# Scores of a neighbourhood attention as three split-format matmuls instead of one in full precision

## The chip, the cores and the metric

The kernel runs on one core of a Trainium2 chip. The metric is the device time of one execution in microseconds (us), as the median of several runs. The engines are named as in the profile: PE (TensorE matmuls), PEld (its weight loads), DVE (VectorE), ACT (ScalarE), POOL (GpSimd), SP (SyncE, which issues most DMAs).

## What is computed

One layer of an encoder on 512 tokens (a grid of 8 rows by 64 columns) with 2048 channels, in float32. The normalised input is projected to five parts: value and gate of a convolution group (group a, 1024 channels), and queries, keys and values of a 2-D neighbourhood attention (16 heads of 64 channels). The outputs of both groups are normalised, projected together and added to the input; a gated FFN of width 5632 follows. The part that the change concerns is

```python
scores = jnp.einsum("bchd,bicjhd->bchij", q_row, k_win).astype(jnp.float32)
scores = scores + jnp.transpose(bias, (2, 0, 1, 3))[None]
p = jax.nn.softmax(scores.reshape(b, GRID_W, h, kh * kw), axis=-1)
return jnp.einsum("bchij,bicjhd->bchd", p, v_win)
```

where a token sees all 8 rows and a window of 16 columns, and q is scaled by 1/8.

## The kernel before

**Layout and products.** Channels lie on the 128 partitions, tokens on the free axis (512). A large product is made in the split format: each factor is the sum of a high part, rounded to the format fp32r, and a low part, and three matmuls hi\*hi, hi\*lo, lo\*hi are added in PSUM (`mm3`, lines 126 to 128, one weight block of 128x128 against 512 tokens). Weights come by DMA in units of 8 blocks (`raw`, 128x1024, seven buffers, issued by SP three units ahead); `parts` makes the high part with ACT (`whi`, line 115) and the low part with DVE (`wlo`, line 116), with four buffers each. So a whi or wlo waits until PE is done with the unit four before, and PE waits for it if it is late.

**Stages.** `ORDER` (line 51, `"aavaav" + "aq" * 4 + "qqqq"`) says what is projected in turn: a pair of value and gate tiles of the convolution ("a"), half of the attention's values ("v"), or queries and keys of one pair of heads ("q", eight pairs). Then `out_half` projects the outputs of group a (products `po2`, shown as po), later those of the attention, and the FFN follows (from about 690 us on). A projected tile takes two weight units of 24 matmuls. After each unit, `tick` (line 133) moves two hand-written generators on by one step: `attention` (line 525) and, from pair 4 on, `group_a` (line 390). The instructions of a step may not be issued before that unit's last matmul. Beyond that and the pinned sequences, the scheduler of the language sets each engine's order when the kernel is built, by priorities and by when it reckons that inputs are ready; each engine then works through its list in that fixed order.

**Attention of a pair** (two heads of 64 channels, on partitions 0 to 63 and 64 to 127). `project_qk` (line 427) projects q and k; DVE empties the PSUM banks, times the token's norm (lines 433 and 437, the latter with the keys in another order of tokens). `scores` (line 465): eight matmuls, four column blocks b by two heads, each contracting 64 rows, with 128 queries against 256 keys, in full precision, pinned one behind the other (line 472; the trace shows each as two instructions). `softmax` (line 479) adds the bias table that a DMA has brought (DVE, line 482), and takes maximum, exponential (ACT, line 487) and quotient (DVE, line 489, `tab`). `turn` transposes the result on PE (line 499, `trp`), ACT empties it (line 504, `pt`). `values` (line 507) multiplies by the values into the PSUM bank with the tag "po"; ACT copies it out as `ao` (line 520) and squares it (`sq`, line 168) for the attention's norm.

**Group a.** `group_a` sums the eight convolved tiles y on DVE (`acc`, line 396), gets the mean by a matmul with ones (`st`, line 399), subtracts it (line 404), normalises twice, and makes the split operands `ma`. `rsqrt_steps` (line 171) makes a token's norm and spreads it over the partitions by two matmuls on diagonal matrices (`st<-dg,ones`, line 218), which ACT copies out (line 220, named after the norm: `ra` for group a's second one). These `st` use the bank "po" too, of which there is one. `read_a` (line 593) empties the first products of `out_half` once `ra` is there: DVE multiplies by it (`oa`, line 598) and adds to the residual (line 599). There are three banks for such products (`psm`, "mm"), so the fourth product waits for the first to be emptied.

Of the kernel before, what the change touches and what calls it, by code (L numbers as in the profile page):

```python
# [10 lines left out]
F32 = mybir.dt.float32  # L11
F32R = mybir.dt.float32r
AF = mybir.ActivationFunctionType
# [3 lines left out]
P = 128  # L17
# [49 lines left out]
def layer(ctx: ExitStack, tc: tile.TileContext, xT, xG, w_in, w_v, w_out, w_up, w_down, par, tab, out):  # L67
    nc = tc.nc
# [16 lines left out]
    def t2(name, dt=F32):  # L85
        return tp.tile([P, S], dt, tag="t2k", name=name)
# [5 lines left out]
    pin = tc.keep_in_program_order  # L92
# [170 lines left out]
    for k in range(KD):  # L263
        x1.append(t2("x"))
        last = pin(nc.sync.dma_start(x1[k], xG[k]))
        h, l = t2("xh", F32R), t2("xl", F32R)
# [35 lines left out]
    def project(n):  # L302
        ps = psm.tile([P, S], F32, tag="mm", name="pj")
        for u in range(KD // U):
            w = weights()
            for k in range(U):
                kk = u * U + k
                m = mm3(ps, w, k, xs[kk][0], xs[kk][1], kk == 0, kk == KD - 1)
            tick(m)
            while late and rstd:  # L310
                late.pop(0)()
        return ps
# [114 lines left out]
    def project_qk(p):  # L427
        got = []
        for j, nm in enumerate("qk"):
            ps = project(2 * NC_ + j * NP_ + p)  # L430
            t = t2(nm)
            if nm == "q":
                nc.vector.tensor_mul(t, ps, rstd[0])
            else:

                by = "p (i j c) -> p j i c"
                nc.vector.tensor_mul(t.rearrange("p (j i c) -> p j i c", i=NB, j=2), ps.rearrange(by, i=NB, j=2),
                                     rstd[0].rearrange(by, i=NB, j=2))
            got.append(t)
        qk.append(got)  # L440

    def keys(k, b):

        if b in (0, NB - 1):
            w = k.rearrange("p (j c) -> p j c", j=2)[:, :, b and P:(b and P) + P]
        else:
            w = k[:, b * 64:b * 64 + 384].rearrange("p (j c) -> p j c", j=2)[:, :, :P]
        return w.rearrange("p j (i c) -> p i j c", i=2)
# [5 lines left out]
    hps = [slice(j * DH, (j + 1) * DH) for j in range(2)]  # L454
# [10 lines left out]
    def scores(p, first):  # L465
        q, k = qk[p]
        wide = psa.tile([P, 2, 2, 2 * P], F32, tag="sc", name="sc")
        banks = [wide[:, j] for j in range(2)]
        banks += [psa.tile([P, 2, 2 * P], F32, tag="tr", name="sc", bufs=2) for _ in range(2)]
        for b in range(NB):  # L470
            for j, hp in enumerate(hps):
                m = nc.tensor.matmul(banks[b // 2 * 2 + j][:, b % 2, :], q[hp, b * P:(b + 1) * P],
                                     keys(k, b)[hp], start=True, stop=True)
                if not first:
                    pin(m)
                first = False
        return banks

    def softmax(banks, ts):
# [45 lines left out]
    def attention():  # L525

        before = None
        for p in range(NP_):
            while len(qk) <= p:
                yield  # L530
            ts = tables(p)
            yield
            if before:
                values(*before)
            banks = scores(p, not before)
            softmax(banks, ts)
            yield
            yield
            yield
            pts = turn(ts)  # L540
            yield
            before = p, pts
        yield
        values(*before)
        yield

    p, n = -1, 0
    for step in ORDER:
        if step == "a":
            if n < 2:  # L550
                with tc.issue_after(last.ins):
                    glu(n)
            else:
                glu(n)
            n += 1
            continue
        if step == "v":
            project_v(len(vg))
            continue
        p += 1  # L560
        project_qk(p)
        if p == 0:
            steps.append(attention())
        if p == NORM_AT:
            asteps.append(group_a())
# [439 lines left out]
```

## Time and profile before

| what | us |
|---|---|
| median of 3 runs | 2044.64 (2043.89 to 2045.69) |
| profiled execution | 2047.1 |
| its span (first to last instruction) | 2045.3 |
| PE busy in it | 2025.5 |
| DVE busy | 1672.8 |
| ACT busy | 1035.4 |
| scores of pair 0 start | 237.7 |
| scores of pair 7 end | about 527 |
| granted clock of TensorE, mean | 0.996 |

The page and its views come from one profiled execution, which is a little longer than the median. A line of a timeline reads: start, duration (both us), engine, line of the kernel, operation, output<-inputs, shape and type, number of instructions; then, in brackets, how long the engine sat idle before it and what it waited for. Of matmuls, which are pipelined, the time from start to start is what one costs; the duration also holds the pipeline's depth. A group line ends with the busy time of the group, the mean duration in ns, and the idle time before its members. A line of windows reads: stretch, its length, busy us and number of instructions for each engine, granted clock (1.00 is full), busy share of the DMA engines, GB/s.

### The profile page before, as it was taken

What the parts mean: (1) busy time and instruction counts of PE and PEld (TensorE: products, weight loads), DVE (VectorE), ACT (ScalarE), POOL (GpSimd) and SP (SyncE); (2) the same over time, 40 slices, a digit from 0 to 9 for tenths busy, and PEclk for the clock granted to TensorE, in tenths of its full rate; (3) what the DMA queues carried; (4) which work ended last, traced back from release to release, by engine and by line L of the source; (5) the groups of instructions that cost most, each with busy time, mean ns of one, the idle gap of its engine ahead of it and who ended that gap; (6) DMA issues with size and microseconds to landing.
All of it is one profiled execution on the core that took longest, in us unless ns stands there. A gap on an engine that the chain in (4) does not pass through costs nothing.

```text
span 2045.3 us, 28399 instructions
## 1 busy us (share of the span) xinstructions
PE 2025.5 (99%) x10752; PEld 1731.9 (85%) x10752; DVE 1672.8 (82%) x2319; ACT 1035.4 (51%) x1662; POOL 156.2 (8%) x186
## 2 busy tenths in 40 slices
PE   9999999999999999999999999999999999999997
PEld 7888888878888898888888888888888888888887
DVE  7986888878577898888888788788888888889876
ACT  6323234347346555555555555555554555555552
POOL 0000000000001001111111111111111111110110
PEclk9999999999999999999999999999999999999998
DMA  7232333336347435566566565665555566555682
GB/s 254 82 104 91 114 95 103 108 119 216 104 121 178 113 114 144 118 151 145 124 144 144 135 133 145 138 134 142 131 146 143 124 146 146 130 134 127 149 212 83
DMA packets 97209, 275.38 MB, mean 135 GB/s; under 512 B 10928, under 2 KB 11696, under 8 KB 97072
## 3 DMA queue, kind: packets, MB, share of 16 engines
q1 hardware_dynamic: 71712, 227.40, 36.6%
q0 software_dynamic: 25216, 46.15, 15.6%
q8 instruction: 85, 1.39, 0.3%
q14 instruction: 52, 0.43, 0.1%
q10 hardware_dynamic: 144, 0.01, 0.0%
HBM read 218.99 MB, written 54.53 MB: 134 GB/s over the span
## 4 chain that ended last, share of the span: by engine, by line
PE 95%; DVE 2%; ACT 1%; DMA 1%; issue 1%; SPq 0%; DVEq 0%; ACTq 0%
PE pu L723 25%; PE pu L728 13%; PE pd L128 8%; PE pd L126 8%; PE pd L127 8%; PE pj L128 5%; PE pj L127 5%; PE pj L126 5%; PE po L126 3%; PE po L127 3%; PE po L128 3%; PE pv L330 1%; PE pv L332 1%; PE pv L331 1%; PE pu L126 1%; PE pu L128 1%
## 5 line engine op out<-in xcount | busy, mean ns | idle before, releaser
L115 ACT ACTIVATE whi<-raw 128x1024 fp32r<-128x1024 f32 x364 | 384.9, 1059 | 506.2 <-PE pj L127 148.0
L116 DVE TENSOR_TENSOR wlo<-raw,whi 128x1024 fp32r<-128x1024 f32 x364 | 443.9, 1221 | 215.6 <-ACT whi L115 205.9
L723 PE MATMUL pu<-xc,whi 128*128 128x512 f32 x2240 | 574.9, 392 | 0.2 <-ACT pl L735 0.2
L723 PEld LDWEIGHTS pu<-xc,whi 128*128 128x128 f32 x2240 | 409.2, 189 | 74.3 <-ACT pl L735 0.5
L728 PEld LDWEIGHTS pu<-xc,wlo 128*128 128x128 f32 x2240 | 305.6, 190 | 21.9
L728 PE MATMUL pu<-xc,wlo 128*128 128x256 f32 x2240 | 312.3, 282 | 0.0
L128 PE MATMUL pd<-hh,wlo 128*128 128x512 f32 x640 | 249.2, 391 | 0.0
L127 PE MATMUL pd<-hl,whi 128*128 128x512 f32 x640 | 249.2, 389 | 0.0
L126 PE MATMUL pd<-hh,whi 128*128 128x512 f32 x640 | 248.9, 391 | 0.0
L842 POOL DMA_DIRECT2D x2d<-pdc x160 | 139.2, 872 | 1169.6 <-ACT pdc L841 1051.5
L127 PE MATMUL pj<-xl,whi 128*128 128x512 f32 x512 | 200.4, 391 | 0.1
L128 PE MATMUL pj<-xh,wlo 128*128 128x512 f32 x512 | 200.0, 391 | 0.0
L126 PE MATMUL pj<-xh,whi 128*128 128x512 f32 x512 | 198.6, 392 | 0.4 <-ACT xh L267 0.4
L735 ACT ACTIVATE pl<-pu 128x256 f32<-128x256 f32 x280 | 104.4, 382 | 168.6 <-PE pu L723 168.5
L115 ACT ACTIVATE whi<-ws 128x1024 fp32r<-128x1024 f32 x132 | 139.6, 1058 | 76.9 <-PE pu L723 55.3
L384 DVE SCALAR_TENSOR_TENSOR y<-ch,prm,y 128x500 f32<-128x500 f32 (+14 forms) x240 | 173.4, 741 | 4.5
L116 DVE TENSOR_TENSOR wlo<-ws,whi 128x1024 fp32r<-128x1024 f32 x132 | 160.8, 1218 | 19.7 <-ACT whi L115 19.6
L128 PEld LDWEIGHTS pd<-hh,wlo 128*128 128x128 f32 x640 | 120.1, 188 | 28.8 <-DVE wlo L116 3.0
L127 PEld LDWEIGHTS pd<-hl,whi 128*128 128x128 f32 x640 | 120.3, 188 | 25.0
L126 PEld LDWEIGHTS pd<-hh,whi 128*128 128x128 f32 x640 | 120.5, 188 | 21.9
L841 ACT ACTIVATE pdc<-pd 128x512 f32<-128x512 f32 x160 | 93.8, 588 | 84.1 <-PE pd L128 84.1
L126 PEld LDWEIGHTS pj<-xh,whi 128*128 128x128 f32 x512 | 96.0, 188 | 22.3 <-issue 1.7
(188 smaller groups left out, 2911.3 us busy)
## 6 DMA issues: line engine op xcount, KB each, us to landing
raw<-in_w_up SPq DMA_DIRECT2D x176, 512.0 KB, 3.7
raw<-in_w_down SPq DMA_DIRECT2D x88, 512.0 KB, 4.0
x2d<-pdc POOLq DMA_DIRECT2D x160, 256.0 KB, 4.8
raw<-in_w_in SPq DMA_DIRECT2D x60, 512.0 KB, 3.7
raw<-in_w_out SPq DMA_DIRECT2D x32, 512.0 KB, 3.7
raw<-in_w_v SPq DMA_DIRECT2D x16, 512.0 KB, 4.0
tab<-in_tab SPq DMA_DIRECT2D x32, 256.0 KB, 5.1
x<-in_xG SPq DMA_DIRECT2D x16, 256.0 KB, 5.3
```

The costliest lines, as they stand in the source:

```text
L115: i = nc.scalar.activation(hi[:, :n], raw[:, :n], AF.Copy)
L116: j = nc.vector.tensor_sub(lo[:, :n], raw[:, :n], hi[:, :n].bitcast(F32))
L126: nc.tensor.matmul(ps, hi[:, a], mh, start=start, stop=False)
L127: nc.tensor.matmul(ps, hi[:, a], ml, start=False, stop=False)
L128: return nc.tensor.matmul(ps, lo[:, a], mh, start=False, stop=stop)
L330: nc.tensor.matmul(ps, xh, wh[:, f], start=kk == 0, stop=False)
L384: nc.vector.scalar_tensor_tensor(y[:, a:b], h[:, a + j - PAD:b + j - PAD], prm[:, o + j:o + j + 1], y[:, a:b], op0=ALU.mult, op1=ALU.add)
L723: return nc.tensor.matmul(ps, w[0][:, k * P:(k + 1) * P], comb[c][k], start=k == 0, stop=k == U - 1)
L728: nc.tensor.matmul(ps[:, H:], w[1][:, k * P:(k + 1) * P], comb[c][k][:, :H], start=False, stop=False)
L735: nc.scalar.activation(to, ps, AF.Copy)
L841: nc.scalar.activation(t, ps, AF.Copy)
L842: nc.gpsimd.dma_start(xd[d], t, accum_op=ALU.add)
```

## The change

After the eviction of q and of k, ACT copies the tile to a high part in fp32r and DVE subtracts it from the tile for a low part (16 copies and 16 subtractions of 128x512 in all). Each score matmul becomes three: high keys by high queries, low keys by high queries, high keys by low queries, added in PSUM. The part is the outer loop, the head the inner, so a pair has 24 matmuls of 64 rows instead of 8 in full precision. Softmax and all else stay as they are. Lines behind the first edit have numbers higher by 3, lines behind the second by 5.

```diff
@@ project_qk
-            got.append(t)
+            h, l = t2(nm + "h", F32R), t2(nm + "l", F32R)
+            nc.scalar.activation(h, t, AF.Copy)
+            nc.vector.tensor_sub(l, t, h.bitcast(F32))
+            got.append((h, l))
         qk.append(got)
@@ scores
         for b in range(NB):
-            for j, hp in enumerate(hps):
-                m = nc.tensor.matmul(banks[b // 2 * 2 + j][:, b % 2, :], q[hp, b * P:(b + 1) * P],
-                                     keys(k, b)[hp], start=True, stop=True)
-                if not first:
-                    pin(m)
-                first = False
+            at = slice(b * P, (b + 1) * P)
+            for part, (x, y) in enumerate(((0, 0), (0, 1), (1, 0))):
+                for j, hp in enumerate(hps):
+                    m = nc.tensor.matmul(banks[b // 2 * 2 + j][:, b % 2, :], q[x][hp, at], keys(k[y], b)[hp],
+                                         start=part == 0, stop=part == 2)
+                    if not first:
+                        pin(m)
+                    first = False
         return banks
```

## The prediction

> **What bounds the kernel now.** I read the page first: how busy each engine is, then the chain that ended last.
>
> ```profile
> span 2045.3 us, 28399 instructions
> ...
> PE 2025.5 (99%) x10752; PEld 1731.9 (85%) x10752; DVE 1672.8 (82%) x2319; ACT 1035.4 (51%) x1662; POOL 156.2 (8%) x186
> ...
> PE 95%; DVE 2%; ACT 1%; DMA 1%; issue 1%; SPq 0%; DVEq 0%; ACTq 0%
> ```
>
> PE is busy for 99% of the span and carries 95% of the chain. So time saved on PE is saved in the end, unless PE then waits for something that was just in time before. DVE at 82% is the likely source of such waits. ACT at 51% is the second, since it runs in a fixed order. The sum is made against the profiled execution (2047.1 us, of which 2045.3 are the span and 1.8 lie around it); it is 2.5 us (0.12%) above the median of 2044.64, so I take the differences from it and put them on the median. About 0.2% (4.1 us) can be told from no change here: faster is under 2040.5, slower over 2048.7.
>
> **1. The scores themselves.** The first fence has PE's timeline around the scores of pair 0, then the view of line 472 by itself. Then come two slices of PE's warm-up (line 258: split-format matmuls of 64 rows, 256 and 512 columns, two halves of the array in turn) and a group row.
>
> ```profile
> 237.35 0.39 PE L128 MATMUL pj<-xh,wlo 128*128 128x512 f32 x1
> 237.67 2.00 PE L472 MATMUL sc<-k,q 64*128 64x256 f32 x16
> 239.60 0.50 PE L126 MATMUL pj<-xh,whi 128*128 128x512 f32 x1
> ```
>
> ```profile
> L472 PE MATMUL sc<-k,q x128: 376/376/480, 237.7 to 526.8; 64*128 64x256 f32 x128
> ```
>
> ```profile
> 5.20:5.32 0.12, 0.12 (x6) 0.12 (x4) 1.00 0.87 341
> 5.32:5.44 0.12, 0.12 (x6) 0.12 (x4) 1.00 1.02 393
> ```
>
> ```profile
> L728 PE MATMUL pu<-xc,wlo 128*128 128x256 f32 x2240 | 312.3, 282 | 0.0
> ```
>
> A pair has 8 matmuls in the program, and the trace shows 16: one in full precision is two instructions. They run as eight groups of two, one for each head, which lie beside each other: (2.00 - 0.48) / 7 = 0.217 us from group to group. The block holds PE for 239.60 - 237.67 = 1.93 us, of which 8 x 0.217 = 1.73 is this cadence and 0.2 is entering and leaving. After the change there are 24 instructions in twelve groups of two. No row shows such a group, so its price is bounded. Split-format 64-row matmuls moved on by one group per 0.12 us in the warm-up; I take 0.119. The line of 128x256 gives 312.3 / 2240 = 0.139 at worst, and half of the old cadence, 0.108, is the other end. So a block takes 12 x 0.119 + 0.2 = 1.63 us: 0.30 less per pair, and 2.4 us over eight pairs (ends: 0.06 less, 0.43 less). I take the warm-up, as it has the same 64 rows and both halves of the array.
>
> The Trainium skill ("FP8 and Floating Point Precision", TensorE Precision Notes) counts four passes for full precision; three instead of four would save a quarter of the 1.73, or 3.5 us in all, by my estimate from that page. The trace gives 0.217 for four passes, 0.054 each, while the warm-up pays 0.119 for one group, so it is against the whole quarter.
>
> **2. The copies and subtractions.** The groups below are the nearest to them; then come a stretch of projections (busy time of PE, PEld, DVE, ACT, POOL) and DVE's timeline.
>
> ```profile
> L267 ACT ACTIVATE xh<-x,g 128x512 fp32r<-128x512 f32 x16 | 11.0, 725 | 3.3 <-DMA x<-in_xG 2.2 <-DMA g<-in_par 1.1
> L268 DVE SCALAR_TENSOR_TENSOR xl<-x,g,xh 128x512 fp32r<-128x512 f32 x16 | 11.2, 749 | 5.5 <-ACT xh L267 5.4
> ```
>
> ```profile
> 200.00:250.00 50.00, 50.00 (x229) 40.98 (x228) 42.24 (x59) 14.41 (x26) 0.00 (x0) 1.00 0.37 111
> ```
>
> ```profile
> 227.37 0.68 DVE L437 TENSOR_TENSOR k<-pj,rstd 128x512 f32<-128x512 f32 x1
> ...
> 418.44 1.22 DVE L116 TENSOR_TENSOR wlo<-raw,whi 128x1024 fp32r<-128x1024 f32 x1 [4.21 <-ACT whi L115]
> ```
>
> Sixteen copies at about 0.7 us on ACT and sixteen subtractions at 0.7 on DVE make 11 us on each, 1.4 per pair. In a 50-us stretch, about a pair, DVE has 7.8 us free and ACT over 30. The scores need the low part of k, but the eviction of k in pair 0 ends at 228.05 and its scores start at 237.67: 9.6 us of cover for a copy and a subtraction. I cost this at nothing. Without the cover, a wait on it would be 1.4 us per pair.
>
> **3. What moves.** In the built program the score blocks and what follows them stand at other places among the weight matmuls. Counting those from the scores of pair 4: the mean of group a (line 399) stands behind 52 of them instead of 49, the scores of pair 5 at 142 instead of 127, the first transposes at 194 instead of 192, the norm of group a (line 218, its second use) behind 288 instead of 280. Up to pair 4, PE has no wait in this stage. Then there were two:
>
> ```profile
> 432.31 0.39 PE L126 MATMUL pj<-xh,whi 128*128 128x512 f32 x1
> 434.02 1.10 PE L399 MATMUL st<-acc,ones 128*128 128x512 f32 x2 [1.32 <-DVE acc L396]
> ...
> 478.87 0.39 PE L127 MATMUL pj<-xl,whi 128*128 128x512 f32 x1
> 480.17 0.63 PE L499 MATMUL trp<-ident,tab 128*128 128x128 f32 x4 [0.91 <-DVE tab L489]
> ...
> 481.77 0.40 PE L128 MATMUL pj<-xh,wlo 128*128 128x512 f32 x1
> ```
>
> ```profile
> 432.46 1.41 DVE L396 TENSOR_TENSOR acc<-acc,y 128x512 f32<-128x512 f32 x2
> ...
> 480.54 1.22 DVE L116 TENSOR_TENSOR wlo<-raw,whi 128x1024 fp32r<-128x1024 f32 x1
> ```
>
> Wait A costs 434.02 - 432.31 - 0.23 = 1.48 us. It ends when DVE has its sum, whatever PE does. Three weight matmuls more ahead of it (3 x 0.227, the time between neighbours) give PE 0.68 us of work that was waiting; pair 4's 0.30 goes into that wait. Wait B costs 480.17 - 478.87 - 0.23 = 1.07; with the scores of pair 5 further back, the transposes have their input in time, and it goes. But at 481.77 a matmul starts just as the wlo of 480.54 ends (481.76): with B gone this weight part is late next, and I put 0.33 on it (bounds 0 and 1.07). The gain ahead of the norm is then 6 x 0.30 + 0.68 + 1.07 - 0.33 = 3.2 us (six pairs, without the fourth). Loads on SP's queue move too: bias tables of pair 6 by two weight loads, x by two; in my walk each still lands before its reader, the tables of pair 6 with the least to spare. I cost that at nothing; if they come late, the transposes of pair 6 are late by as much.
>
> **4. The new wait, C.** Here the norm of group a moves, on PE and against ACT's queue. PE, then ACT, then DVE, in before:
>
> ```profile
> 502.62 0.64 PE L218 MATMUL st<-dg,ones 128*128 128x512 f32 x2
> 503.10 0.40 PE L127 MATMUL po<-mal,whi 128*128 128x512 f32 x1
> ...
> 504.49 0.40 PE L127 MATMUL po<-mal,whi 128*128 128x512 f32 x1
> ...
> 504.95 0.39 PE L126 MATMUL po<-mah,whi 128*128 128x512 f32 x1
> ```
>
> ```profile
> 498.96 1.06 ACT L115 ACTIVATE whi<-raw 128x1024 fp32r<-128x1024 f32 x1 [1.10 <-PE po L127]
> 499.93 0.49 ACT L487 ACTIVATE tab<-tab,nm 128x256 f32<-128x256 f32 x1
> ...
> 501.90 0.58 ACT L520 ACTIVATE ao<-po 128x512 f32<-128x512 f32 x1
> ...
> 503.30 0.60 ACT L220 ACTIVATE ra<-st 128x512 f32<-128x512 f32 x1 [0.15 <-PE st L218]
> 504.92 1.06 ACT L115 ACTIVATE whi<-raw 128x1024 fp32r<-128x1024 f32 x1 [1.03 <-PE po L127]
> ```
>
> ```profile
> 503.93 1.29 DVE L598 TENSOR_TENSOR oa<-po,ra 128x512 f32<-128x512 f32 x2
> ```
>
> The norm's matmuls (st) write the one bank that ACT's ao (line 520) empties, and in before that was done 0.14 us ahead (502.48 against 502.62). ACT then made ra, DVE used it to empty a product bank (503.93 and half of 1.29: 504.6), and the matmul at 504.95 that needed the bank came 0.35 later. All margins just held. In the built after, ACT's order is turned: the whi of 504.92, which waits for the matmul of 504.49, stands ahead of ao, sq and ra, not behind them. And st stands one matmul behind the one that this whi waits for; directly behind st comes the matmul that needs the emptied bank. Let T be the time at which st would start (504.95 by before's clock). whi starts at T - 0.03; the next on ACT 0.97 later (498.96 to 499.93), so ao ends at T + 0.94 + 0.58 = T + 1.52. st starts 0.14 later at T + 1.66, ra 0.68 behind it (502.62 to 503.30) and ends at T + 2.94, oa needs 0.03 + 0.69, and PE goes on at about T + 3.8. Undisturbed it would be T + 0.48 (502.62 to 503.10). The wait costs 3.3 us: the lead of 3.2 is gone, and pair 7's 0.30 is left.
>
> **5. The clock.** PE's work is thin for these 3.8 us: two idle stretches of 1.7 with two matmuls between them. Something like it is in before, at the start of the FFN:
>
> ```profile
> 691.06 0.28 PE L128 MATMUL pu<-xc,wlo 128*128 128x256 f32 x1
> 692.47 1.01 PE L218 MATMUL st<-dg,ones 128*128 128x512 f32 x2 [1.14 <-DVE dg L213]
> 694.17 0.39 PE L126 MATMUL pu<-xc,whi 128*128 128x256 f32 x1 [0.69 <-ACT rstd L220]
> ```
>
> ```profile
> 692.00:696.00 4.00, 2.79 (x12) 0.82 0.21 80
> 696.00:700.00 4.00, 4.00 (x28) 0.75 0.00 0
> ```
>
> (The last rows: busy PE, granted clock, DMA.) Behind it the granted clock was 0.5 for (0.18 + 0.25) x 4 / 0.5 = 3.4 us, worth at most half of that, 1.7 us. At waits A and B, shorter, the clock stayed at 1.00. C is the longer kind, so I expect such a stretch and take 1.5 us (ends: 0 and 1.7).
>
> The Trainium skill ("TensorE: Matmul & The Clock Gate", Part 1) has the clock drop after one idle window of about 3.4 us. The trace shows a drop with gaps of 1.14 and 0.69 around two matmuls; a wholly idle window isn't needed.
>
> **The sum:** -3.2 - 0.3 + 3.3 + 1.5 = +1.3: 2044.64 + 1.3 = **2046.0 us** (span 2046.6, profiled 2048.4).
>
> **Rivals.**
> - *C without a drop of the clock*: 2044.64 - 0.2 = 2044.5. For it: the two gaps of C are split by two matmuls, as idle stretches A and B were short. Against it: the drop at 694. By the skill's rule on a wholly idle window it would be this one.
> - *C doesn't bite*: ACT runs early enough, or the chip's margins at the norm differ from my walk. Then the lead stays: 2044.64 - 3.5 = 2041.1, and with the low cadence (12 x 0.011 x 8 = 1.1 more) 2040.0, which is faster. Against it: whi waits for PE's own progress, so no lead of PE's changes the order.
> - *The heads do not lie side by side* in the new groups, which is the slower side: 24 instructions one after the other at 0.119 are 2.86 instead of 1.43 us per pair, 11.4 us in all: 2057. It is slower than before from 0.149 us per group on (2.9 us over 96 groups beyond 0.119); at 0.139 the time is 2047.9. Speaking for it: each group has its own weights to load, 24 per pair instead of 16. Against it: the warm-up's slices.
>
> **How the numbers follow.** C with the clock: 0.40, 2046.0. C without: 0.25, 2044.5. C not biting: 0.17, about half of it under 2040.5. Slower groups, or a wait that I have not found, over 2048.7: 0.18. So faster 0.09, same 0.40 + 0.25 + 0.08 = 0.73, slower 0.18. The range reaches from C not biting with the low cadence (2040.0) to the forecast with 0.139 (+1.9), the dearest clock (+0.2) and the weight part's bound (+0.7): 2040.0 to 2048.8; it leaves out some 0.18.
>
> **What would show it.** In after: a score block of 24 instructions that lasts 1.6 us; no waits of scores on the low parts; wait A shorter by 0.7, B gone; at the second st (line 218 there too) an idle time of about 1.7 us that ao ends, then one of 1.6 that oa ends; and a slice with a granted clock under 1 behind it. The prediction is wrong if the block takes 2 us or more, if st doesn't wait for ao, or if PE waits at places that have none now.

## The result, and the profile after

On one chip the kernel before took 2045.68 us (median of 12 runs, 2043.89 to 2046.76) and the changed kernel 2049.78 (12 runs, 2045.52 to 2052.68). The ratio is 1.0018, with an interval of 1.001 to 1.0026. The change makes the kernel slower, by some 4 us. As a ratio that is a little under the 0.2% below which the prediction spoke of no change, but the interval excludes 1, and the time lies over the 2048.7 from which it spoke of slower, and 1.0 us above the upper end of the range. Of the 3.8 us between the forecast of 2046.0 and this time, 1.0 lies in the base: the three runs that the prediction started from have a median of 2044.64, the twelve here one of 2045.68. The runs of the changed kernel spread over 7 us, those of the kernel before over 3: that is a finding too, and it comes back below.

The profiled execution took 2052.57 us; so it is one of the longer ones. Two lines of its page, the span and the chain by engine:

```profile
span 2050.8 us, 28563 instructions
...
PE 93%; DVE 3%; DMA 2%; issue 1%; ACT 1%; DVEq 0%; ACTq 0%
```

PE still carries nearly all of the chain, but the DMAs' share went from 1% to 2%. The span is 2050.8 - 2045.3 = 5.5 us longer than before. To see where this arises, I followed the same matmuls through both traces. PE's timeline at the scores of pair 0:

```profile
237.37 0.39 PE L477 MATMUL sc<-kh,qh 64*128 64x256 f32 x2
237.59 0.28 PE L477 MATMUL sc<-kl,qh 64*128 64x256 f32 x2
237.71 0.28 PE L477 MATMUL sc<-kh,ql 64*128 64x256 f32 x2
...
238.78 0.28 PE L477 MATMUL sc<-kh,ql 64*128 64x256 f32 x2
238.99 0.50 PE L126 MATMUL pj<-xh,whi 128*128 128x512 f32 x1
```

Each score row is a group of two, one matmul for each head. There are twelve, and from the second to the last it is (238.78 - 237.59) / 10 = 0.119 us from group to group. The block holds PE for 238.99 - 237.37 = 1.62 us, against 1.93 before. (This execution is 0.30 us ahead here already; that is its start, not the change.) The waits of PE between 400 and 540 us, all of them (in total, times, longest):

```profile
PE po L126 <- DVE oa L603: 1.4, 1, 1.4
PE st L218 <- ACT ao L525: 1.4, 1, 1.4
PE st L399 <- DVE acc L396: 0.9, 1, 0.9
```

Wait A is 0.9 us instead of 1.3, wait B is gone, and two new ones stand at the place called C. PE's timeline there, then ACT's, one row of DVE's and two windows (PE, PEld, DVE, ACT, POOL, clock, DMA):

```profile
500.30 0.39 PE L127 MATMUL po<-mal,whi 128*128 128x512 f32 x1
...
502.32 0.73 PE L218 MATMUL st<-dg,ones 128*128 128x512 f32 x2 [1.41 <-ACT ao L525]
504.47 0.50 PE L126 MATMUL po<-mah,whi 128*128 128x512 f32 x1 [1.41 <-DVE oa L603]
...
505.53 0.63 PE L126 MATMUL po<-mah,whi 128*128 128x512 f32 x1
505.95 0.63 PE L127 MATMUL po<-mal,whi 128*128 128x512 f32 x1
```

```profile
500.73 1.06 ACT L115 ACTIVATE whi<-raw 128x1024 fp32r<-128x1024 f32 x1 [0.20 <-PE po L127]
501.69 0.58 ACT L525 ACTIVATE ao<-po 128x512 f32<-128x512 f32 x1
...
503.09 0.60 ACT L220 ACTIVATE ra<-st 128x512 f32<-128x512 f32 x1 [0.16 <-PE st L218]
```

```profile
503.72 1.28 DVE L603 TENSOR_TENSOR oa<-po,ra 128x512 f32<-128x512 f32 x2
```

```profile
502.00:506.00 4.00, 2.27 (x7) 1.49 (x8) 4.00 (x7) 1.50 (x3) 0.00 (x0) 0.87 1.06 396
506.00:508.00 2.00, 2.00 (x6) 1.60 (x5) 1.50 (x3) 0.00 (x0) 0.00 (x0) 0.50 0.78 303
```

The matmul of 500.30 ran at 504.49 before: 4.19 us ahead, of which 0.48 is the norm that before had already done and 0.30 the earlier start, so the lead is 3.4. Then whi, ao, st, ra, oa follow one another as the prediction walked them. The matmul of 504.47 ran at 504.95 before: 0.2 us of the lead is left. Behind it neighbours are 0.42 apart instead of 0.23, at half the clock, and behind pair 7's scores the lead has turned into a lag:

```profile
528.07 0.50 PE L126 MATMUL po<-mah,whi 128*128 128x512 f32 x1
```

That matmul started at 527.12 before, so the lag is 0.95 us, or 1.25 without the earlier start; the prediction's sum has 1.3. From here to 633 us every engine runs 0.95 behind. The rest, 5.5 - 0.95 = 4.5 us, arises at the start of the FFN, for which the prediction's sum has no term. DVE's timeline there, before and then after:

```profile
633.34 1.23 DVE L673 TENSOR_TENSOR ws<-raw 128x1024 f32<-128x1024 f32 x1
```

```profile
636.32 1.23 DVE L678 TENSOR_TENSOR ws<-raw 128x1024 f32<-128x1024 f32 x1 [2.06 <-DMA raw<-in_w_up]
```

`ws` is the first sum of two weight blocks of the FFN. It reads a load that SP issues. SP's timeline and the DMA view (KB, us from issue to landing) of this one load, before and then after:

```profile
628.39 0.33 SPq L110 DMA_DIRECT2D raw<-in_w_up  x1
```

```profile
raw<-in_w_up SPq DMA_DIRECT2D x1, 512.0 KB, 4.9
```

```profile
629.34 0.33 SPq L110 DMA_DIRECT2D raw<-in_w_up  x1
```

```profile
raw<-in_w_up SPq DMA_DIRECT2D x1, 512.0 KB, 6.9
```

Before, the load landed at 633.3, just as DVE came to it at 633.34: a margin of less than 0.1 us, which no row of waits shows, as the row has no idle time. After, it took 2 us more. Behind `ws` on DVE stand the low parts `xc` of the FFN's input and a low weight part. DVE itself has slack here: before, it waited 7.8 us for PE between 628 and 690 us, after only 2.5. But SP issues a next load only when DVE has made the weight part that frees the buffer. The next load of these weights left at 643.23 instead of 640.25, and DVE's waits for such loads grew (in total, times, longest; before and then after):

```profile
DVE raw L675 <- DMA raw<-in_w_up: 1.2, 2, 0.6
```

```profile
DVE raw L680 <- DMA raw<-in_w_up: 5.5, 2, 2.8
```

So DVE's lag of 3.0 us lasts up to the last `xc`, for which PE waited 0.77 us in before already. The matmul that waits is the 44th of the FFN; the first starts at 674.20 before (so the FFN begins there, and not at about 690) and at 675.14 after. PE, before and after, and the windows of after:

```profile
680.28 0.39 PE L126 MATMUL pu<-xc,whi 128*128 128x256 f32 x1 [0.77 <-ACT xc L612]
```

```profile
683.32 0.58 PE L126 MATMUL pu<-xc,whi 128*128 128x256 f32 x1 [2.86 <-ACT xc L617]
```

```profile
682.00:686.00 4.00, 2.68 (x12) 2.68 (x13) 3.22 (x10) 3.15 (x9) 0.00 (x0) 0.55 0.84 212
686.00:690.00 4.00, 4.00 (x24) 4.00 (x23) 3.88 (x4) 1.95 (x5) 0.00 (x0) 0.59 0.17 58
```

The lag is 683.32 - 680.28 = 3.04 us. Behind this wait the clock was halved for (0.45 + 0.41) x 4 / 0.5 = 6.9 us, which is worth at most 3.4; matched matmuls lag by 5.6 behind it, and what follows gives back 0.7 and takes again 0.5. Up to the last 20 us this execution ran at half clock for 13.7 us in all (3.4 behind C, 6.8 here, 3.4 behind 699), that of the kernel before for 3.4.

### The profile page after: what moved, and what is told of

It is laid out like the page before. It is cut to its first block, busy times and chain, and to the rows that moved or that the text cites. A ratio compares the mean times of both kernels' runs of the same rounds, so it can differ in the third digit from the quotient of the medians.

```text
span 2050.8 us, 28563 instructions
## 1 busy us (share of the span) xinstructions
PE 2027.6 (99%) x10816; PEld 1735.9 (85%) x10816; DVE 1681.5 (82%) x2335; ACT 1046.1 (51%) x1678; POOL 156.6 (8%) x186
## 4 chain that ended last, share of the span: by engine, by line
PE 93%; DVE 3%; DMA 2%; issue 1%; ACT 1%; DVEq 0%; ACTq 0%
PE pu L728 25%; PE pu L733 13%; PE pd L128 8%; PE pd L126 8%; PE pd L127 8%; PE pj L126 6%; PE pj L128 6%; PE pj L127 6%; PE po L126 2%; PE po L128 2%; PE po L127 2%; DMA raw<-in_w_up 2%; PE pv L332 1%; PE pv L331 1%; PE pv L330 1%; PE pu L126 1%
```

## The experiments

Two theories stood at first. **M**: the prediction's mechanism (C and the clock behind it) takes the lead, and this is the whole of what is regular. **L**: the load at the FFN's start is late because of the change, and its wait is the larger part. Each batch ran on one chip beside runs of the kernel before. Diffs are against the changed kernel unless said otherwise.

### e1: the changed kernel again

> The changed kernel once more, not altered, to see how its time spreads and what its profile shows when it is short. Theory M (the moved order makes the wait C and a stretch of half clock behind it; what comes on top is a load of FFN weights that lands late in some executions): runs fall in two groups, about 2045 to 2047 and 2048 to 2053. If this profile is of the short group, C is there all the same (two gaps of 1.4 us at the second st), but the first pu matmul of the FFN waits about 1 us instead of 2.9. Rival L (the loads land late always, because of the change): the wait of 2.9 is there in any profile.

Measured: 2046.14 us (11 runs, 2043.25 to 2053.3) against 2045.21 (28 runs); ratio 1.0009, 1.0 to 1.0018. Of its profile, the window at C, the load, and PE's wait for `xc`:

```profile
500.00:510.00 10.00, 7.18 (x25) 5.22 (x24) 6.89 (x11) 2.77 (x4) 0.00 (x0) 0.83 0.74 280
```

```profile
raw<-in_w_up SPq DMA_DIRECT2D x1, 512.0 KB, 4.3
```

```profile
PE pu L126 <- ACT xc L617: 0.7, 1, 0.7
```

C and the clock are there with the same gaps (PE busy 7.18 of 10 us); the load is in time and the wait at the FFN is what it was before. This execution took 2047.47 us, without a late load. So C belongs to the kernel, while the late load is something that happens in some executions: L in its strict form falls.

### e2: before with the copies and subtractions alone

```diff
+            h, l = t2(nm + "h", F32R), t2(nm + "l", F32R)
+            nc.scalar.activation(h, t, AF.Copy)
+            nc.vector.tensor_sub(l, t, h.bitcast(F32))
             got.append(t)
```

(Against before; the scores stay in full precision.)

> Only the copies and subtractions are added; the scores stay in full precision, and nothing reads the new tiles. The built order turns at C as with the whole change (whi ahead of ao, st behind 288 weight matmuls). Theory M: C costs its two gaps of about 1.4 us here too, and no score gain pays for it: 8 x 0.31 = 2.5 us slower than the whole change in the same state, 2048 to 2055, and 2 to 8 us over before. Rival S (the three matmuls are what costs): no slower than before, within 1 us.

Measured: 2051.41 us, ratio 1.0031 (1.002 to 1.0043). PE's waits between 400 and 540 us:

```profile
PE st L218 <- ACT ao L523: 3.0, 1, 3.0
PE po L126 <- DVE oa L601: 1.4, 1, 1.4
...
```

C is there, and bigger, without any change of a matmul. It is 5.3 us longer than e1 beside it: the scores' 2.4 us are missing and the first gap is 1.6 longer; the rest wasn't followed up.

### e3: the three matmuls alone

```diff
-            t = t2(nm)
+            t = t2(nm, F32R)
-            got.append(t)
+            got.append((t, t))
```

(Against before, with the change's new loop in `scores`. q and k are rounded to the high part at their eviction and all three matmuls multiply high parts: the low parts are left out, and scores come out three times too large.)

> Only the scores are changed: q and k are evicted straight into fp32r and the three matmuls all take this high part (the low parts are left out, so the scores are coarser). No copy, no subtraction. The built order is that of before at C (ao, sq, ra, then whi). Theory M: no gaps at C, the gain of the scores stays, 8 x 0.31 = 2.5 us, less up to 1 us at the second st, where ao's chain on DVE and ACT now has less lead: 2 to 3 us under before, 2042.5 to 2044. Rival S: as slow as the whole change, or slower than before.

Measured: 2044.15 us, ratio 0.9996 (0.9987 to 1.0005). PE's timeline:

```profile
501.10 0.62 PE L218 MATMUL st<-dg,ones 128*128 128x512 f32 x2
...
503.14 0.50 PE L126 MATMUL po<-mah,whi 128*128 128x512 f32 x1 [0.95 <-DVE oa L600]
```

The norm doesn't wait for ao at all: ACT's order is that of before. The lead runs into a wait of 0.95 for oa. So C comes with the copies, not with the matmuls. Yet with the matmuls alone the gain is only 1.1 us, not the 2 to 3 expected, and can't be told from none.

### e4 and e5: the norm's work moved up

```diff
-RA_AFTER = 5
+RA_AFTER = 4
```

(e4: group a's second norm is asked for one product sooner. e5: beside that, the third low weight part behind the first oa may not be issued before it, by the lines below; `gate` holds that oa twice.)

```diff
-        j = nc.vector.tensor_sub(lo[:, :n], raw[:, :n], hi[:, :n].bitcast(F32))
+        held = gate.pop() if gate else None
+        with tc.issue_after(held.ins) if held and not gate else nullcontext():
+            j = nc.vector.tensor_sub(lo[:, :n], raw[:, :n], hi[:, :n].bitcast(F32))
```

> The whole change, with RA_AFTER 4 instead of 5: the second norm of group a is asked for one weight unit earlier, and in the built order its st stands behind 247 and 249 weight matmuls, ahead of pair 5's values, so it does not wait for ao, and ra is ready before whi. Theory M: both gaps of C and its half clock go; the lead of about 3.5 us over before stays up to the FFN: 2041 to 2043. If the late loads come by chance or by the change itself (rival L), some runs are 2 to 6 us longer even so; if they came from C's shift of the phase, none are. Rival W (the added work on DVE and ACT costs by itself): no more than 1 us better than the whole change.

> The whole change with RA_AFTER 4 and one pinned place: the third wlo behind the first oa must be issued behind that oa on DVE. In the built order the first oa then stands ahead of everything on DVE that waits for the weight unit ending at 288. The run with RA_AFTER 4 alone still waited 4.4 us at matmul 289, for oa, which stood on DVE behind the wlo whose whi waits for that unit. Theory M2 (a wait of PE on ACT and DVE work that is queued behind a whi or wlo released by PE's own last unit): the wait at 289 goes, no half clock behind it, the lead of 3.5 to 4 us lasts to the FFN: short runs of 2041 to 2043, a tail up to 5 us longer where FFN loads land late. Rival W (the added DVE and ACT work costs by itself): no better than 2046.

Measured: e4 2047.95 us (ratio 1.002, 1.0011 to 1.0029), e5 2047.7 (1.0016, 1.0007 to 1.0025). Both expectations failed. PE's timeline in e4, then in e5 PE's and DVE's:

```profile
505.57 0.80 PE L126 MATMUL po<-mah,whi 128*128 128x512 f32 x1 [4.38 <-DVE oa L603]
```

```profile
506.03 0.56 PE L130 MATMUL po<-mah,whi 128*128 128x512 f32 x1 [4.23 <-DVE oa L607]
```

```profile
504.69 0.69 DVE L498 TENSOR_TENSOR tab<-tab,su 128x512 f32<-128x512 f32 x1
505.30 0.68 DVE L607 TENSOR_TENSOR oa<-po,ra 128x512 f32<-128x512 f32 x1
```

The norm is early now, but oa is still late: in e5 it stands on DVE behind the quotients of pair 6's softmax (line 498), no longer behind a weight part. So no single neighbour holds it; something puts oa late in DVE's order wherever the norm is.

### e6 and e7: the FFN's first sums on POOL

```diff
+        add = nc.gpsimd.tensor_add if f == 0 else vadd
...
-    add = nc.vector.tensor_add
+    add = vadd = nc.vector.tensor_add
```

(e7: the same, together with e5.)

> The whole change, and the additions of the first FFN weight unit's factors (ws and raw, lines 678 to 689) made by POOL instead of DVE. The wait C stays as it is. Theory L1 (the long runs come from DVE standing still at that addition until a weight load has landed, which makes xc late, then PE's first FFN matmul, then the clock): a late load no longer holds up DVE, the wait ahead of the first pu matmul is 1 us or less in all runs, and the runs over 2048 go: median about 2045.5 to 2046.5, none over 2048.5. Rival L2 (long runs come from elsewhere, the clock for instance): as many runs over 2048 as without.

> Both of these together. Theories M2 and L1: 2041 to 2043 in all runs, faster than before by 2 to 4 us and under both kernels. If only M2 holds: as the first of this call with its tail. If only L1 holds: about 2045.5 without a tail.

Measured: e6 2051.28 us (ratio 1.0033), e7 2053.85 (1.0044, 1.0031 to 1.0056). Worse, and both expectations failed: the load landed 7.7 us after its issue in e6's profile, another instruction of DVE waited for such a load as well (3.5 us), and POOL's sum took 2.5 us. In e7's profile the load was in time (4.1 us), and PE waited 3.5 us for `xc` all the same. That DVE's place for `ws` is the only thing wrong at the FFN isn't borne out.

### e8: the changed kernel a third time

> The changed kernel once more on this chip, beside the three above, for their comparison and for one more profile. Theory: two groups of runs again, 2043 to 2047 and 2048 to 2053; the profile has C's two gaps of 1.4 us. If it is a long run, DVE waits for a load of in_w_up of about 2 us ahead of the FFN, and the first pu matmul waits about 3 us instead of 1; if it is short, neither.

Measured, in the batch of e5 to e7: 2050.56 us, ratio 1.0026 (1.0015 to 1.0037). Its window at C, then waits at the FFN's start:

```profile
500.00:510.00 10.00, 7.18 (x24) 5.15 (x23) 6.55 (x11) 2.77 (x4) 0.00 (x0) 0.83 0.76 286
```

```profile
PE pu L126 <- ACT xc L617: 2.5, 1, 2.5
...
DVE ws L678 <- DMA raw<-in_w_up: 2.4, 1, 2.4
```

C, the clock and the late load (7.3 us), as in the first profile. Only the drop of the clock behind the FFN's wait for `xc` is absent. This execution took 2047.94 us, the shortest of the seven, in spite of the late load.

### e9, e10 and e11: the residual's loads spread out

All tiles of 128x512 come from one pool of 79 places. The change asks it for 32 more in all, four for each pair. Ahead of `out_half` the program takes 16 places for the residual x at once (`x2`), and `oa` takes its places behind them. Theory **P**: with these in use, x2, oa and what follows get places later, and therefore the scheduler puts ao, ra and oa late in ACT's and DVE's order; C is a matter of room. The test takes six x2 tiles ahead and one more per product:

```diff
-    for d in range(KD):
-        xk = t2("x2")
-        nc.sync.dma_start(xk, xT[d])
-        x2.append(xk)
+    def load_x(n):
+        for d in range(len(x2), min(n, KD)):
+            x2.append(t2("x2"))
+            nc.sync.dma_start(x2[d], xT[d])
+
+    load_x(6)
...
         for d in range(KD):
+            load_x(d + 6)
```

(e9: the changed kernel with it. e10: also `RA_AFTER = 4`. e11: before with it, as the control.)

> The whole change, but the 16 loads of the residual x2 are issued six at first and then one for each product of out_half, instead of all at once; so up to ten tiles of the pool of 79 are free for longer. Theory P (what turned the order at C are the 32 added tiles: x2 and oa wait for a place in the pool, and the scheduler lets whi and softmax pass): in the built order whi no longer stands between the exponentials and ao, st stands behind 273 instead of 288 weight matmuls, and oa comes sooner. The wait C shrinks from 2.8 us in two gaps to under 1.5, no half clock behind it: short runs of 2042 to 2044.5. Rival W (the added copies and subtractions cost by their time on the engines): as the whole change, 2046 or more.

> The same with RA_AFTER 4, so that ra does not wait for ao. The first oa then stands on DVE ahead of most of pair 6's softmax and of the wlo that waits for the unit ending at 288. Theory P with this place: no wait at matmul 289, the lead of about 4 us lasts to the FFN: short runs of 2041 to 2042.5, long ones (late FFN load) up to 5 us more. Rival W: 2046 or more.

> The kernel before with the same late loads of x2, without the change: what they are worth by themselves. Theory: before has no wait at C, so little is to be had; within 1 us of before. If it gains 2 us or more, the gain of the two runs above is not that of the score matmuls.

Measured, all beside the kernel before at 2045.67 us (33 runs): e9 2042.24, ratio 0.9985 (0.9976 to 0.9994); e10 2042.12, ratio 0.9983 (0.9974 to 0.9992); e11 2045.72, ratio 1.0001 (0.9992 to 1.001). ACT in e9, then e10's window at C's place:

```profile
496.65 0.58 ACT L525 ACTIVATE ao<-po 128x512 f32<-128x512 f32 x1
...
499.20 0.58 ACT L220 ACTIVATE ra<-st 128x512 f32<-128x512 f32 x1
499.68 1.05 ACT L115 ACTIVATE whi<-raw 128x1024 fp32r<-128x1024 f32 x1
```

```profile
500.00:510.00 10.00, 10.00 (x54) 8.26 (x53) 10.00 (x19) 7.11 (x20) 0.00 (x0) 1.00 0.42 148
```

ao and ra stand ahead of whi again, PE is busy for all of 500 to 510 us at full clock, and C's two waits are gone in both, so the lead stays. The same edit gives before nothing. So the lead is real and worth 3.4 to 3.6 us. What took it is not the time of the copies and subtractions, which are all still there, but the order that came with them. That this order turned for want of room is argued from theory P: the edit changes both the places that are held and the moments at which x is loaded, and a larger pool alone wasn't tried. Both versions beat the kernel before beside them; e10's runs spread over 2.8 us (2040.36 to 2043.13), no more than before's. In e9's profile (2045.58 us, one of its two longest) the load for the FFN still took 7.4 us, PE waited 2.0 us for `xc`, and the clock fell behind that.

### e12: fewer accumulating DMAs

```diff
-        else:
-            nc.gpsimd.dma_start(sq2[d % 2], q, accum_op=ALU.add)
```

(14 of the 16 squares of the FFN's norm are left out, so its norm comes from two tiles of 16.) POOL issues one of these DMAs 0.15 us ahead of the load that comes late (629.19 and 629.34; 628.25 and 628.39 before).

> The whole change, but of the squares of x2 only the first two tiles are stored; the other 14 accumulating DMAs on POOL's queue are left out (so the FFN's norm is made from 2 of 16 tiles). C stays. Theory L3 (the load of FFN weights at about 629 us lands late where it shares the DMA engines with those accumulating DMAs, issued 0.15 us apart): the loads of 600 to 680 us land in 4 to 5 us each, the first pu matmul waits about 1 us, and the long runs go: all of 2045 to 2047. Rival L2 (the clock alone makes the long runs): as many runs over 2048 as without.

Measured, in the batch of e9: 2045.1 us, ratio 1.0 (0.9991 to 1.0009). Its load, and PE's waits between 400 and 700 us but for two that stand in before as well:

```profile
raw<-in_w_up SPq DMA_DIRECT2D x1, 512.0 KB, 4.6
```

```profile
PE po L126 <- DVE oa L603: 1.4, 1, 1.4
PE st L218 <- ACT ao L525: 1.4, 1, 1.4
...
PE pu L126 <- ACT rstd L220: 0.7, 1, 0.7
```

C is unchanged and the wait for `xc` is gone; over the runs nothing is left of the kernel's lag. But one profile with the load in time doesn't show that these DMAs make it late, as e1's load was in time beside them, and e1's interval (from 1.0) reaches this ratio. And the long runs did not all go, though theory L3 expects it: three of eleven took 2047.57 to 2048.73 us. (The DMAs that are left out may be worth something elsewhere too; that wasn't separated.)

### e13 to e16: is the late load the change's?

Three single executions of before and one of after, on one chip.

> The kernel before, for one more profile. If late loads come by chance in both kernels (theory L), one look in two or three has the load of about 628 us land in 6.5 us or more, and DVE's ws waits about 2 us for it; such a look is 1.5 to 2.5 us longer than one without. If the change brings them about (rival), the load lands in 4 to 5 us in each look.

> The same kernel, second look, same expectation: load of about 628 us in 6.5 us or more in one look of two or three by theory L, in 4 to 5 us by the rival.

> The same kernel, third look, same expectation: load of about 628 us in 6.5 us or more in one look of two or three by theory L, in 4 to 5 us by the rival.

> The changed kernel beside them, for a fourth profile: C's gaps of 1.4 and 1.4 us; a time of about 2046 if the load of about 629 us lands in under 5 us, of 2048 to 2053 if it takes 6.5 us or more.

Measured: before 2043.71, 2044.57 and 2046.94 us, after 2045.79. e16's window at C, its load, DVE's wait and PE's:

```profile
500.00:510.00 10.00, 7.18 (x33) 5.29 (x32) 6.86 (x11) 3.17 (x5) 0.00 (x0) 1.00 0.76 285
```

```profile
raw<-in_w_up SPq DMA_DIRECT2D x1, 512.0 KB, 6.5
```

```profile
DVE ws L678 <- DMA raw<-in_w_up: 1.7, 1, 1.7
```

```profile
PE pu L126 <- ACT xc L617: 1.2, 1, 1.2
```

The expectation for e16 failed: with a load of 6.5 us it was to take 2048 to 2053 us. The load was late, but PE waited only 1.2 us for `xc`, the clock fell neither at C nor behind that wait, and the time is a short one.

The load took 4.9, 4.6, 4.9 and 4.8 us in the four profiles of before, 5.0 in e11 and 4.8 in e3, which has no copies; in the four of the changed kernel 6.9, 4.3, 7.3 and 6.5. Of all eleven profiles with the copies and the accumulating DMAs, six have it at 5.7 us or more (after, e5, e6, e8, e9, e16) and five at 4.0 to 5.1 (e1, e2, e4, e7, e10). In e16 it was issued at 627.39, in e13 at 627.46: the moment of the issue doesn't make the difference. So a late load was seen only with the copies, in about half of the profiles.

## Why the prediction was wrong

Step by step, in the prediction's order:

- **The scores.** Right: 0.119 us per group and 1.62 for the block, predicted 0.119 and 1.63. The heads do lie side by side. (The limit from which the rival is slower is 0.147 us per group, 2.7 us over 96 groups; the prediction has 0.149.)
- **The copies and subtractions at nothing.** Right for their time, since nothing waits on the low parts. Wrong for what they bring: e2 and e3 show that C comes with them, and e9 to e11 that it goes when the loads of x are spread, with all of them still there. The prediction took C from the built order and had it as a matter of that order; it didn't ask why ACT's order turned.
- **The lead.** Predicted 3.2 us, measured 3.4, in part by luck: wait A is shorter by 0.4 instead of 0.7, and the late weight part, put at 0.33, didn't come, so two misses cancel. B is gone as predicted.
- **C.** The place, both releasers and the price are as predicted: 3.4 - 0.2 = 3.2 us against 3.3. The two gaps are 1.41 each, not 1.7 and 1.6.
- **The clock.** In the first profile the matmuls go from 0.48 us ahead (504.47) to 0.95 behind (528.07); with pair 7's gain of 0.3 on top, the stretch cost 1.7 us, against 1.5 with an end at 1.7. But it isn't a property of the gaps: e1 and e8 have the drop, e16, the same kernel, has the same two gaps and none (a clock of 1.00), and so has e12. So the forecast and the rival without the clock were one case with two outcomes. Nor is the row on which the prediction built this term a fixed price: the drop at 694 in before is there again in e15, and absent in e13 and e14 behind the same gaps.
- **The sum.** The step that failed is here, and with it the size of the clock's term. The sum -3.2 - 0.3 + 3.3 + 1.5 ends at 527 us, and what was behind it was taken to move along unchanged. Up to 633 us that held, with +0.95 against the forecast 1.3. The part on what moves looked at SP's loads only up to pair 6's tables; the first loads of the FFN, with a margin of nothing in before, were not among them. There a load that lands 2 us later, and a drop of the clock behind the wait, made +0.95 into +5.5. In the sum's terms: the wait for `xc` is 2.9 us instead of 0.8, where the sum has nothing, and the half clock is 13.7 us long instead of 3.4, worth at most 5.1 us more, where the sum has 1.5. It is the "wait that I have not found" in the case with 0.18, but no number was worked out for it, and no term or bound of the range stood for it. The margin of under 0.1 us could be read from the trace of before; that the load would be late could not, and how often the clock would fall could not be read from one profile.

Which of the two weighs more is in the profiles of the two kernels side by side (half clock: the time at a granted clock of 0.50 up to the last 20 us; us):

| profile | load | PE's wait for `xc` | half clock | time |
|---|---|---|---|---|
| before, first | 4.9 | 0.8 | 3.4 | 2047.1 |
| before, e13 | 4.6 | 0.6 | 0 | 2043.71 |
| before, e14 | 4.9 | 0.7 | 0 | 2044.57 |
| before, e15 | 4.8 | 0.8 | 3.4 | 2046.94 |
| after, first | 6.9 | 2.9 | 13.7 | 2052.57 |
| after, e1 | 4.3 | 0.7 | 6.8 | 2047.47 |
| after, e8 | 7.3 | 2.5 | 6.8 | 2047.94 |
| after, e16 | 6.5 | 1.2 | 3.4 | 2045.79 |

A microsecond at half clock costs at most half of one. Take that away, and the four executions of before lie at 2043.7 to 2045.4 us, those of after at 2044.1 to 2045.7. The time goes with the half clock, and not with the load alone.

The mean granted clock of every run bears it out. Beside e1 it is 0.9968 for before and 0.9959 for the changed kernel, so 6.5 and 8.4 us of time are lost at most; the means of the times differ by 1.9. Beside e8 it is 0.9968 and 0.9943, so 6.6 and 11.7 us; the times differ by 5.5. By this upper estimate under 0.1 and 0.4 us are left for all else. (For the first batch the clock of before is not on record.) The 30 runs of the changed kernel in these three batches lie between 2043.25 and 2053.3 us, ten of them at or below 2046.61, around the forecast; before's lie between 2043.62 and 2047.31. So the forecast is about the time of the executions in which the clock falls seldom, and the median is one with more. That the waits at C and for `xc` are what lets it fall is argued: all stretches at half clock that the eight profiles show up to the last 20 us lie at C, at the wait for `xc`, or at the norm's two gaps at the FFN's start, and e9 and e10, which lack C, have none at its place.

**What stays open** is why the load is late in about half of the profiles with the copies and in none without. The load and the accumulating DMA are issued 0.15 us apart in both kernels, and the sequence of DMAs there is the same; whether these DMAs are needed for the delay e12 doesn't settle, and a shift in time alone doesn't do it (e13 and e16). An earlier issue of this load wasn't tried. Open too is why the same gaps are followed by half the clock in one execution and not in another.

## What to carry to other kernels

An edit that is free in engine time can still cost by the order that it brings about on other engines, here probably by the tiles that it holds: count them against the pool, and look at which loads and evictions get their place later. Where a lead of PE is to survive, follow it to the end of the kernel, and look for the inputs that land just when their reader comes; they have no row among the waits, and a slower transfer there can reach PE (2.1 us here). A drop of the clock behind a gap, read from one profile, is one outcome and not a price: take a second profile before putting it into a sum. Where a lead is lost, ease the suspected resource in the changed kernel and, as a control, in the kernel before: here it brought 3.5 us in the one and nothing in the other.

## What the runs showed of the hardware

- Three split-format matmuls of 64 rows cost 3 x 0.119 = 0.357 us for the two heads together, against 2 x 0.217 = 0.434 for the full precision's (both by two heads side by side, 256 columns): 18% less, not a quarter.
- Up to the last 20 us, half the clock came in stretches of 3.4 us, or of 6.8, and the same gaps brought it in one execution and not in another. Two idle stretches of 1.41 us with two matmuls between them were followed by it in three profiles of this kernel (after, e1, e8: 0.83 over 500 to 510 us) and not in e12 and e16 (1.00), with the same 7.18 us of PE at work. Gaps of 1.14 and 0.69 us were followed by it in two profiles of the kernel before and not in e13 and e14. A wait of 2.9 us (after) and one of 2.0 (e9) were followed by half the clock, one of 2.5 us was not (e8). The Trainium skill ("TensorE: Matmul & The Clock Gate", Part 1) has the clock watched over a window that runs freely; that the same gaps fall differently into it would fit, while its drop after one wholly idle window does not.
- A load of 512 KB issued 0.15 us behind an accumulating DMA on POOL's queue landed after 4.0 to 7.7 us (4.6 to 5.0 in the six profiles without the copies); with most of those DMAs taken away, after 4.6 in the one profile.
